# Average pooling of 33.55 MB: 2 KB per partition of the output stored from ScalarE's queue among the last loads

## The chip, the cores and the metric

The kernel runs on one core of one Trainium2 chip. The metric is device time in microseconds (us). A ratio is the mean time of one kernel's fast runs over that of the other's of the same rounds, so it is not quite the ratio of the medians that are quoted beside it.

## The reference

```python
def setup_inputs():
    batch, channels, d, h, w = (8, 32, 32, 32, 32)     # float32, kernel_size = 2
...
    for i, j, k in ...:                                # 16 x 16 x 16 windows
        window = x[:, :, 2*i:2*i+2, 2*j:2*j+2, 2*k:2*k+2]
        result[:, :, i, j, k] = np.mean(window, axis=(-3, -2, -1))
```

(The three loops are drawn together here.) The input is 33.55 MB, the output 4.19 MB. Each number is read once and takes part in one average, so the work is mostly movement.

## The kernel before

The 256 pairs of batch and channel are two halves (t = 0, 1) of 128 partitions. In each half a partition reads 128 KB and writes 16 KB. VectorE adds planes, then neighbours in a row, then rows, and scales by 1/8.

```python
    plan = [
        (0, 0, (32,)), (0, 32, (32,)), (0, 64, (32,)), (0, 96, (32,)),
        (1, 0, (32,)), (1, 32, (32,)), (1, 64, (16, 16)), (1, 96, (16, 16)),
    ]                                  # half, start in KB, sizes in KB per partition
...
    for t, k0, parts in plan:
        tin = pool_in.tile([P, 32 * KF], F32, tag="tin", name="tin")     # 5 buffers
        ...
            nc.sync.dma_start(out=v, in_=xv[...])       # 4 MB, or two of 2 MB ("half loads")
        for v, k, kb in views:
            pool_unit(v, t, k, kb)                      # three VectorE passes into obuf[t]

    for t, k0, kb in [(0, 0, 16), (1, 0, 14), (1, 14, 2)]:               # KB per partition
        nc.sync.dma_start(
            out=ov[t * P:(t + 1) * P, k0 * KF:(k0 + kb) * KF],
            in_=obuf[t][:, k0 * KF:(k0 + kb) * KF])
```

(The plan is set in fewer lines than in the source.) All ten loads and all three stores are issued by SyncE, on one queue. The closing part of the kernel, not shown, waits for the stores one by one.

Of the kernel before, what the change touches and what calls it, by code (L numbers as in the profile page):

```python
# [1 line left out]

# [4 lines left out]

F32 = mybir.dt.float32
KF = 256


@with_exitstack
def pool_rows(
    ctx: ExitStack,
    tc: tile.TileContext,
    x: bass.AP,
    kernel_size: int,
    out: bass.AP,
):
    nc = tc.nc  # L20
    assert kernel_size == 2, "only kernel_size == 2 supported"

    B, C, D, H, W = x.shape
    P = nc.NUM_PARTITIONS
    assert (B * C, D, H, W) == (2 * P, 32, 32, 32)
    add = mybir.AluOpType.add



    xv = x.rearrange("b c d h w -> (b c) (d h w)")  # L30
    ov = out.rearrange("b c d h w -> (b c) (d h w)")




    pool_in = ctx.enter_context(tc.tile_pool(name="pin", bufs=5))
    pool_out = ctx.enter_context(tc.tile_pool(name="pout", bufs=1))
    obuf = [pool_out.tile([P, 16 * KF], F32, name=f"obuf{t}") for t in range(2)]
    dummy = pool_out.tile([P, 1], F32, name="dummy")


    plan = [
        (0, 0, (32,)),
        (0, 32, (32,)),
        (0, 64, (32,)),
        (0, 96, (32,)),
        (1, 0, (32,)),
        (1, 32, (32,)),
        (1, 64, (16, 16)),
        (1, 96, (16, 16)),  # L50
    ]

    def pool_unit(buf, t, k0, kb):

        od = kb // 8
        a = buf.rearrange("p (o dd e) -> p o dd e", o=od, dd=2)
        b = buf[:, :od * 1024]
        nc.vector.tensor_add(  # L58
            out=b.rearrange("p (o e) -> p o e", o=od), in0=a[:, :, 0], in1=a[:, :, 1])
        bv = b.rearrange("p (e ww) -> p e ww", ww=2)  # L60
        c = buf[:, od * 1024:od * 1536]
        nc.vector.tensor_add(out=c, in0=bv[:, :, 0], in1=bv[:, :, 1])  # L62
        cv = c.rearrange("p (j hh k) -> p j hh k", hh=2, k=16)
        o0 = k0 * KF // 8
        nc.vector.tensor_tensor_reduce(  # L65
            out=obuf[t][:, o0:o0 + od * 256].rearrange("p (j k) -> p j k", k=16),
            in0=cv[:, :, 0], in1=cv[:, :, 1],
            scale=0.125, scalar=0.0, op0=add, op1=add, accum_out=dummy[:, :],
        )

    for t, k0, parts in plan:
        tin = pool_in.tile([P, 32 * KF], F32, tag="tin", name="tin")
        views = []
        o = 0
        for kb in parts:
            v = tin[:, o * KF:(o + kb) * KF]
            nc.sync.dma_start(
                out=v, in_=xv[t * P:(t + 1) * P, (k0 + o) * KF:(k0 + o + kb) * KF])
            views.append((v, k0 + o, kb))
            o += kb  # L80
        for v, k, kb in views:
            pool_unit(v, t, k, kb)


    for t, k0, kb in [(0, 0, 16), (1, 0, 14), (1, 14, 2)]:
        nc.sync.dma_start(
            out=ov[t * P:(t + 1) * P, k0 * KF:(k0 + kb) * KF],
            in_=obuf[t][:, k0 * KF:(k0 + kb) * KF],
        )


def kernel(tc: tile.TileContext, x: bass.AP, kernel_size: int, out: bass.AP):
    nc = tc.nc
    pool_rows(tc, x, kernel_size, out)
    tc.close()
    tc.compile()  # L96
    blocks = nc.main_func.blocks



    opening, program = blocks[0].instructions, blocks[tc.starting_block_idx].instructions
    load = next(i for i in program if isinstance(i, mybir.InstDMACopy))
    assert load.engine == nc.sync.engine
    barrier = next(
        n for n, i in enumerate(opening)
        if i.engine == load.engine and isinstance(i, mybir.InstDrain))
    program.remove(load)
    opening.insert(barrier, load)




    closing = blocks[-1].instructions
    stores = [
        i for i in program
        if isinstance(i, mybir.InstDMACopy) and "out_" in i.outs[0].memref]
    kept = [u.id for i in stores for u in i.sync_info.on_update]
    final = next(
        i for i in closing
        if i.engine == nc.sync.engine and isinstance(i, mybir.InstDrain))  # L120
    waits = {w.id: w for w in final.sync_info.on_wait}
    closing[closing.index(final)] = mybir.InstDrain(
        name=final.name, engine=final.engine, ins=[], outs=[], is_reset_sema=False,
        sync_info=mybir.SyncInfo(
            on_wait=[w for n, w in waits.items() if n not in kept], on_update=[]))


    reset = next(
        n for n, i in enumerate(closing)
        if isinstance(i, mybir.InstDrain) and i.is_reset_sema)  # L130
    first, stop = closing[reset].reset_range_start, closing[reset].reset_range_stop
    assert isinstance(closing[reset + 1], mybir.InstISA)
    while len(closing) > reset:
        closing.pop()
    n = first
    while n < stop:
        m = n
        while m < stop and m not in kept:
            m += 1
        if m > n:  # L140
            closing.append(mybir.InstDrain(
                name=nc.get_next_instruction_name(), engine=nc.gpsimd.engine, ins=[], outs=[],
                is_reset_sema=True, reset_range_start=n, reset_range_stop=m))
            nc.gpsimd.sem_clear(range(n, m))
        n = m + 1
    for n in kept:
        w = waits[n]
        closing.append(mybir.InstEventSemaphore(
            name=nc.get_next_instruction_name(), engine=nc.sync.engine, ins=[], outs=[],
            sync_info=mybir.SyncInfo(  # L150
                on_wait=[w],
                on_update=[mybir.SyncUpdate(
                    sync_type="semaphore", id=n, ant_name=w.ant_name,
                    update_mode="sem-sub-imm", update_value=w.wait_value)])))


# [1 line left out]
_INS = ['x', 'kernel_size']  # L158
_OUTS = [((8, 32, 16, 16, 16), 'float32')]

_NUMBERS = {'kernel_size': 2}


# [26 lines left out]
```

## Time and profile before

| what | value | where it is read |
|---|---|---|
| time | 91.97 us (91.76 to 92.02, 3 runs); 91.93 with the later ones (6 runs) | the runs |
| span of instructions | 86.4 us | head of the profile |
| transfer queue busy | 99.2% of 16 engines | queue table |
| VectorE busy | 74% | head of the profile |
| last store lands | 85.2 + 5.4 = 90.6 us | issues of the stores |

The span is the time from the first to the last instruction. A transfer goes on after the instruction that issues it, so the kernel ends later than its span. The prediction shows the lines themselves.

### The profile page before, as it was taken

Reading aid. Unit: us, or ns where it says so; the run is one execution under the profiler, and the core shown is the slowest. Engines: PE = TensorE matmul, PEld = TensorE weight load, DVE = VectorE, ACT = ScalarE, POOL = GpSimd, SP = SyncE. Lnnn points to the kernel's source line nnn. Section 1 sums busy time; section 2 is a strip of 40 time slices with the busy share of each in tenths; the row PEclk is TensorE's granted clock in tenths of the full one; section 3 lists DMA queues with packets and bytes.
Section 4 is the critical chain, followed back from the end, with each engine's and each line's share of the span. In section 5 each row is a group of like instructions: output and inputs, shape, how many; then the busy total and the mean of one; then the engine's idle time right before and its main releaser. Section 6 shows DMA issues by size and latency. Waiting matters only on the chain.

```text
span 86.4 us, 90 instructions
## 1 busy us (share of the span) xinstructions
DVE 64.0 (74%) x40; POOL 0.2 (0%) x4
## 2 busy tenths in 40 slices
DVE  0000039993999749993999749992999999999994
POOL 0000000000000000000000000000000000000000
DMA  8979997999979999799979999799999999998999
GB/s 243 425 319 470 486 470 319 425 486 486 455 319 440 486 486 410 319 486 486 470 319 425 486 486 440 304 470 387 455 402 455 395 455 410 440 425 319 448 432 408
DMA packets 1634, 36.37 MB, mean 421 GB/s; under 512 B 176, under 2 KB 176, under 8 KB 176
## 3 DMA queue, kind: packets, MB, share of 16 engines
q1 hardware_dynamic: 1634, 36.37, 99.2%
HBM read 33.55 MB, written 4.19 MB: 437 GB/s over the span
## 4 chain that ended last, share of the span: by engine, by line
DMA 61%; DVE 37%; issue 0%; DVEq 0%
DMA tin<-in_x_dram 61%; DVE tin L58 21%; DVE tin L62 11%; DVE obuf L65 6%; DVE dummy L65 0%; DVEq L96 0%
## 5 line engine op out<-in xcount | busy, mean ns | idle before, releaser
L58 DVE TENSOR_TENSOR tin<-tin 128x4096 f32<-128x4096 f32 (+1 forms) x10 | 35.7, 3569 | 20.6 <-DMA tin<-in_x_dram 20.6
L62 DVE TENSOR_TENSOR tin<-tin 128x2048 f32<-128x2048 f32 (+1 forms) x10 | 18.6, 1864 | 0.3
L65 DVE CUSTOM_DVE_ANT_1 obuf<-tin 128x1024 f32<-128x1024 f32 (+1 forms) x10 | 10.1, 1011 | 0.3
L65 DVE DVE_READ_ACCUMULATOR2_ANT dummy<- 128x1 f32 x10 | 0.8, 82 | 0.0
L171 POOL MEMSET const-bfloat16-1.0<- 128x1 bf16 x1 | 0.1, 102 | 0.0
L171 POOL MEMSET const-uint8-127<- 128x1 uint8 x1 | 0.1, 101 | 0.0
L171 POOL MEMSET const-float32-1.0<- 128x1 f32 x1 | 0.1, 99 | 0.0
L171 POOL MEMSET const-float32-0.0<- 128x1 f32 x1 | 0.1, 98 | 0.2 <-issue 0.2
## 6 DMA issues: line engine op xcount, KB each, us to landing
tin<-in_x_dram SPq DMA_DIRECT2D x6, 4096.0 KB, 34.9
tin<-in_x_dram SPq DMA_DIRECT2D x4, 2048.0 KB, 38.0
out_dram<-obuf SPq DMA_DIRECT2D x1, 2048.0 KB, 36.4
out_dram<-obuf SPq DMA_DIRECT2D x1, 1792.0 KB, 9.1
out_dram<-obuf SPq DMA_DIRECT2D x1, 256.0 KB, 5.4
```

Of the source, the lines that this page charges most:

```text
L58: nc.vector.tensor_add(out=b.rearrange("p (o e) -> p o e", o=od), in0=a[:, :, 0], in1=a[:, :, 1])
L62: nc.vector.tensor_add(out=c, in0=bv[:, :, 0], in1=bv[:, :, 1])
L65: nc.vector.tensor_tensor_reduce(out=obuf[t][:, o0:o0 + od * 256].rearrange("p (j k) -> p j k", k=16), in0=cv[:, :, 0], in1=cv[:, :, 1], s ...
L171: nc = _bacc.Bacc("TRN2", target_bir_lowering=False, num_devices=1)
```

## The change

A quarter of the second half's output is finished near 59 us but leaves only behind all loads, after 85 us. The intent is to let 2 KB per partition of it go at once, by another queue, while the loads still run, and so have that much less to store at the end.

```diff
-    for t, k0, kb in [(0, 0, 16), (1, 0, 14), (1, 14, 2)]:
-        nc.sync.dma_start(
+    for queue, t, k0, kb in [
+        (nc.scalar, 1, 0, 2),
+        (nc.sync, 0, 0, 16),
+        (nc.sync, 1, 2, 12),
+        (nc.sync, 1, 14, 2),
+    ]:
+        queue.dma_start(
...
     kept = [u.id for i in stores for u in i.sync_info.on_update]
+    kept = [n for j, n in enumerate(kept) if n not in kept[j + 1:]]
```

The last line takes doubles out of the list of semaphores that the closing part waits for. Here the four stores have four different semaphores, so it changes nothing.

## The prediction

> **What bounds the kernel now.** I read first the head of the page, because it says whether anything is idle for long, and what.
>
> ```profile
> span 86.4 us, 90 instructions
> DVE 64.0 (74%) x40; POOL 0.2 (0%) x4
> DMA packets 1634, 36.37 MB, mean 421 GB/s; under 512 B 176, under 2 KB 176, under 8 KB 176
> q1 hardware_dynamic: 1634, 36.37, 99.2%
> ```
>
> The one transfer queue is busy for 99.2% of what sixteen transfer engines can give over the span; VectorE (DVE) is busy for 74%. So bytes are the first suspect, though the chain of work that ended last speaks of VectorE near the end. Of its 39 pieces the big ones are these (start, duration, what):
>
> ```profile
> 20.15 40.47 DMA tin<-in_x_dram
> 60.63 0.02 issue
> 60.65 4.44 DVE tin L58
> ...
> 81.01 2.21 DVE tin L58
> 83.22 0.02 issue
> 83.25 1.24 DVE tin L62
> 84.48 0.02 issue
> 84.50 0.69 DVE obuf L65
> 85.20 0.01 DVEq L96
> ```
>
> Until 60.63 us the loads hold the chain, and from 60.65 to 85.20 VectorE works without a pause. This is not yet the end. The span closes with the last instruction, at 86.4 us, but that instruction only issues a store. Next, therefore, the issues of the stores (KB each, us from issue to landing), and when they are issued (in the chain and the timeline: 49.27, 81.0 and 85.2 us):
>
> ```profile
> out_dram<-obuf SPq DMA_DIRECT2D x1, 2048.0 KB, 36.4
> out_dram<-obuf SPq DMA_DIRECT2D x1, 1792.0 KB, 9.1
> out_dram<-obuf SPq DMA_DIRECT2D x1, 256.0 KB, 5.4
> ```
>
> They land at 49.27 + 36.4 = 85.7, 81.0 + 9.1 = 90.1 and 85.2 + 5.4 = 90.6 us. The measured 91.97 us is 1.4 us past that last landing. So the end is set by a transfer. Is that transfer late because its data were late, or because others stand before it? Adding issue and landing of the ten loads in the same way (narrow windows of the loads' tile) gives landings at 12.1, 21.8, 31.5, 41.2, 50.9, 60.6 for the six of 4 MB and 65.5, 70.4, 75.3, 80.8 for the four halves. That is one 4 MB load per 9.72 us: 4.194 MB / 9.72 us = 431.5 GB/s, without a step between them. The stretches towards the end show the same (us, DVE busy, POOL busy, clock, DMA share, GB/s):
>
> ```profile
> 60.00:65.00 5.00, 4.35 (x1) 0.00 (x0) 1.00 1.01 429
> 65.00:70.00 5.00, 4.96 (x4) 0.00 (x0) 1.00 1.00 426
> 75.00:80.00 5.00, 4.93 (x5) 0.00 (x0) 1.00 1.03 393
> 80.00:85.00 5.00, 4.90 (x6) 0.00 (x0) 1.00 0.99 425
> 86.00:88.00 2.00, 0.00 (x0) 0.00 (x0) 1.00 1.00 430
> 88.00:89.00 1.00, 0.00 (x0) 0.00 (x0) 1.00 0.88 377
> 89.00:90.00 1.00, 0.00 (x0) 0.00 (x0) 1.00 0.69 266
> ```
>
> The DMA share stays at 1.0 from the first load to 88 us, loads and stores alike, and falls only in the last two. The queue works strictly in order: the first store, ready at 49.27, waits behind all loads and lands 4.9 us after the last of them. The whole kernel is a single stream of 33.55 + 4.19 = 37.75 MB. Check: 37.75 MB / 431.5 GB/s = 87.5 us, plus a head of 12.1 - 9.7 = 2.4 us, is 89.9, and the rest up to 90.6 is the thinner end of the last store. **The bound is the byte stream, to the very end**; VectorE runs beside it.
>
> **What the Trainium skill says.** "DMA: Bandwidth & Descriptors", section "Issuing engines are not separate DMA queues": DMAs begun by different engines end up on the same 16 DMA engines and interleave; a second issuer saves only the time of issuing. The trace before has one queue alone and can't show it, but it shows that issuing costs little: a store's instruction takes 332 to 347 ns. The same page, "Where 436 GB/s comes from", puts the ceiling at 435.2 GB/s; my 431.5 GB/s is 99% of it, so the trace agrees and leaves no room for an overlap. The same page, "Queues, rings and completion order": each DMA engine takes turns between its queues, a packet at a time. No run so far shows it; I use it for where the moved bytes land in the stream. "Perfetto Trace Analysis", section "DMA Instruction — HWDGE (DVE, Sync)": the profiled window of such an instruction leaves out the movement of data. The trace agrees: about 0.34 us for the first store's instruction, 36.4 us to its landing.
>
> **The change, part by part.** The order of instructions of the changed kernel shows VectorE's forty instructions as before, the same ten loads, one new transfer of 128x512 on ScalarE, and SyncE's second store cut from 128x3584 to 128x3072. Semaphores shift by one slot; the new slots' earlier owners are loads 3, 4 and 5, which land at 41.2, 50.9 and 60.6, before the stores are due at 49.3, 81.0 and 85.2. So no new wait there.
>
> *Removed*: 2 KB from each of the second store's 128 rows. Each of the sixteen engines has eight rows: 8 x 2 KB = 16.4 KB at 431.5/16 = 27.0 GB/s is **0.61 us less** in the tail.
>
> *Added*: 128 packets of 2 KB on ScalarE's queue. What does such a packet cost? The last store is made of them. From 88 us to the end the trace has 187 packets of 0.65 MB, at 39.8% of 16 engines over 4 us = 25.5 engine-us. By bytes these are 27 rows of 14 KB, 128 of 2 KB and 32 tiny ones (completions). The 27 take 27 x 0.53 = 14.4, which leaves 11.1 for the rest; in 89.9 to 90.3 us, 12 packets, seven of them of 2 KB, take 0.63. The two together give about 85 ns per 2 KB and 8 ns per completion. Eight per engine: 8 x 0.085 + 0.008 = **0.69 us more**, as an estimate from these windows.
>
> *Moved*: this store waits for the unit that ends at about 58.95 us, so it is issued at 59.0 and its packets start near 60.5 (the first load's packets appear some 1 us after its issue). From there it stands between the packets of the half loads. A 16 KB row takes 0.61 us, so eight turns of 0.61 + 0.085 are 5.6 us: it should land at about 66.5, some 6 to 9 us after issue. The half loads land 0.6 to 0.7 us later, at about 66.2, 71.1, 76.0 and 81.5. VectorE wants them at 67.32, 72.54, 76.73 and 80.93 (its adds in the timeline): the first three still come in time, and the fourth makes it wait 0 to 0.6 us. The last store is then issued at 85.2 to 85.8. The queue ahead of it has work until some 89 us, so this delay is hidden as well.
>
> *Sum on the stream that sets the end*: -0.61 + 0.69 = +0.08 us; a fourth store's completion to wait for in the closing part, already there by then, about 0.02 us (the small "issue" pieces of the chain). 91.97 + 0.10 = 92.07. What was taken out of the tail has been put in front of it, in the same stream.
>
> **The rivals.** *A: the store is hidden among the loads.* Reads and writes of device memory may use different paths, so the 256 KB would ride for free and the tail be 0.6 us shorter: 91.97 - 0.61 = 91.4. For it: this seems to be the intent, and the tail is all stores while the middle is all loads, so the profile shows no mixed stretch. Against it: loads alone (429) and stores alone (425 to 430) run at the same rate with the share at 1.0, which looks like a limit of the engines and not of a direction. I give it 15 to 20%.
>
> *B: the mixing costs.* Short writes between long reads may slow the reads, or the turns between queues leave gaps. If the 4.9 us that the store spends among loads ran at 393 GB/s, the slowest stretch seen, instead of 429, it would lose 4.9 x (429/393 - 1) = 0.45 us: 92.5. Against it: the page shows no gap at the seams between DMAs. 10 to 15%.
>
> *C: VectorE becomes the bound.* The fourth half load has only 0.1 us of slack, so delays pass into VectorE's chain and the last store. The end moves only if that store's packets come to the engines after the stream has run dry near 89 us. A store that starts moving 1.0 to 1.5 us after issue must be issued after 87.5; that takes 2.3 us of delay, more than three times the estimate. If it did happen, each further us would count in full. 5%.
>
> **Range and chances.** The sum gives 92.07; A pulls a little below it, so I say **92.0 us**. The range goes from A with a little more (91.3) to B in full with some scatter (92.6); the three runs of before span 0.26 us. A change of 2% is 1.84 us, three times all the bytes that are moved, so faster by over 2% has 1%, slower by over 2% has 2% (C, or a cost of the second queue outside the profile), and within 2% has **97%**.
>
> **What would show it right or wrong.** Right: a second queue with 144 packets and 0.26 MB in the profile; the new store landing 6 to 9 us after an issue near 59 us; half loads landing 0.6 to 0.7 us later, VectorE's last unit starting up to 0.6 us later and the span longer by as much (86.4 to 87.1 us), yet the time the same; the DMA share at 1.0 up to some 88 us. Were A right, the half loads would land when they did before, with more than 435 GB/s for a while after 60.5 us, and the last landing would come near 90.0. Were B right, the stretches from 60 to 70 us would show under 420 GB/s with both queues in them. The prediction is wrong if the last landing moves from 90.6 us by more than 0.6 us either way.

## The result, and the profile after

The changed kernel takes **91.77 us** (91.55 to 91.79, 6 runs) against 91.93 us (91.76 to 92.09, 6 runs). The ratio is 0.9979, with a 95% interval from 0.9962 to 0.9995: the same at 2%, and perhaps 0.2% better.

The head and the queue table of the profile after:

```profile
span 86.6 us, 91 instructions
DMA packets 1774, 36.48 MB, mean 421 GB/s; under 512 B 192, under 2 KB 192, under 8 KB 320
q1 hardware_dynamic: 1630, 36.22, 98.4%
q10 hardware_dynamic: 144, 0.26, 0.8%
```

The second queue is there with the 144 packets expected: 128 rows and 16 completions. Mean rate and span are nearly those of before. Next the issues of the stores after (KB, us from issue to landing); the timeline has the issues at 49.3, 81.1, 59.0 and 85.5 us:

```profile
out_dram<-obuf SPq DMA_DIRECT2D x1, 2048.0 KB, 36.8
out_dram<-obuf SPq DMA_DIRECT2D x1, 1536.0 KB, 8.8
out_dram<-obuf ACTq DMA_DIRECT2D x1, 256.0 KB, 9.9
out_dram<-obuf SPq DMA_DIRECT2D x1, 256.0 KB, 4.9
```

ScalarE's store lands at 59.0 + 9.9 = 68.9 us. The other three land at 86.1, 89.9 and 90.4 us, where they landed at 85.7, 90.1 and 90.6 before. So the first store is 0.4 us later and the end is 0.2 us earlier, and the time follows the end. The four half loads land at 66.2, 71.3, 76.2 and 81.2 us, which is 0.6, 0.9, 0.9 and 0.4 us later than before. The chain of work that ended last says the same of the fourth:

```profile
39.96 41.20 DMA tin<-in_x_dram
...
81.18 2.30 DVE tin L58
```

VectorE now waits for this half load, until 81.18 us, where before it was never idle after 60.65 us. Last, the stretches (us, DVE busy, POOL busy, clock, DMA share, GB/s):

```profile
60.00:65.00 5.00, 4.33 (x1) 0.00 (x0) 1.00 1.03 411
65.00:70.00 5.00, 4.97 (x4) 0.00 (x0) 1.00 0.97 412
75.00:80.00 5.00, 4.93 (x5) 0.00 (x0) 1.00 1.02 429
88.00:89.00 1.00, 0.00 (x0) 0.00 (x0) 1.00 0.97 412
89.00:90.00 1.00, 0.00 (x0) 0.00 (x0) 1.00 0.64 244
```

Where ScalarE's store runs, the rate fell from 429 and 426 to 411 and 412 GB/s. From 75 to 80 us it rose from 393 to 429 GB/s. That second difference was not foreseen: no byte was taken out of this stretch.

**Packet records.** The trace also has the start and duration of every packet. One packet is one row of one partition, and every store or load has eight rows on each of the 16 engines. The usual (median) durations are the same in both kernels:

```
row of  2 KB    84 ns        row of 14 KB   535 ns
row of 12 KB   460 ns        row of 16 KB   611 to 613 ns
completion       9 ns
```

The 16 KB rows are not all alike. In the kernel before, 35 of them take 41 to 568 ns longer than the 612 ns, and all of these start between 76.9 and 79.1 us, in the last half load. I add up what every 16 KB row takes over 612 ns and divide by 16; I call this the **excess** per engine. Before it is 0.61 us, nearly all in that slow stretch. After it is 0.40 us: 0.32 between 60 and 64 us and only 0.07 near 78 us.

So the experiments had to settle three things: whether the gain is real, whether it comes from bytes that ride for nothing, from the cut of the store, from the second queue, or from the slow stretch, and what the slow stretch hangs on.

### The profile page after: what moved, and what is told of

Same layout as the page of the kernel before. It is cut to its first block, busy times and chain, and to the rows that moved or that the text cites. A ratio compares the mean times of both kernels' runs of the same rounds, so it can differ in the third digit from the quotient of the medians.

```text
span 86.6 us, 91 instructions
## 1 busy us (share of the span) xinstructions
DVE 64.1 (74%) x40; POOL 0.2 (0%) x4
## 4 chain that ended last, share of the span: by engine, by line
DMA 83%; DVE 14%; SPq 1%; issue 0%; DVEq 0%
DMA tin<-in_x_dram 83%; DVE tin L58 8%; DVE tin L62 4%; DVE obuf L65 2%; SPq L77 1%; DVE dummy L65 0%; DVEq L102 0%
```

## The experiments

Four theories. **Same stream**: what leaves the tail costs as much among the loads. **Partly hidden**: reads and writes overlap a little. **Ends better**: shorter rows or two queues make the tail more even. **Slow stretch**: the gain is a slow stretch of reads that has become smaller. All kernels gave correct results. In the fences from here on, each line is one stretch with the columns as above.

### before_again: the kernel before against itself

> The kernel before against itself: shows what five rounds can resolve, and gives a second trace of it. All theories: ratio 1.000, interval within 0.2% of 1. 'Scatter' theory: the stretch of slow read packets between 77 and 79 us (0.59 us per engine in the first trace) is of another size or place in this trace, and the last landing shifts with it by up to 0.4 us. 'Own property' theory: the stretch is there again, same place, same size.

91.99 us (6 runs) against 92.04 us, ratio 0.9991, interval 0.9971 to 1.0011.

```profile
75.00:80.00 5.00, 4.93 (x5) 0.00 (x0) 1.00 1.00 380
```

The slow stretch is there again: excess 0.63 us, from 76.8 us on, and the last landing is again at 90.6 us. It belongs to this kernel. Five rounds resolve about 0.2%.

### after_again and after_third: the changed kernel repeated

> The changed kernel repeated. 'Same stream' theory (moved bytes cost in the loads what they save in the tail): ratio 0.999 to 1.002, the 0.998 of the first measurement was scatter. 'Partly hidden' theory and 'ends better' theory (the tail of the stores ends more evenly): 0.998 again, with the interval clear of 1. In the trace: half loads again 0.5 to 0.9 us later, last landing 0.1 to 0.3 us earlier.

> The changed kernel a third time, for its ratio and a third trace. 'Slow stretch' theory: ratio 0.997 to 0.999; the trace's excess in 16 KB packets (0.39 us per engine at 91.76 us, 0.61 at 91.96) goes with this profiled run's time, about 0.2 us of time per 0.2 us of excess. 'Same stream' alone: 0.999 to 1.001, no such relation.

Measured: 91.81 us against 92.04, ratio 0.9972 (0.9954 to 0.9990); and 91.90 us against 91.99, ratio 0.9991 (0.9974 to 1.0008), this one on another chip. Of the first repetition, then of the second:

```profile
60.00:65.00 5.00, 4.42 (x1) 0.00 (x0) 1.00 0.96 406
...
75.00:80.00 5.00, 4.93 (x5) 0.00 (x0) 1.00 1.02 387
```

```profile
60.00:65.00 5.00, 4.21 (x1) 0.00 (x0) 1.00 0.99 387
...
75.00:80.00 5.00, 4.93 (x5) 0.00 (x0) 1.00 1.00 429
```

Two of three measurements have intervals clear of 1, and the third leans the same way: a gain of 0.1 to 0.3%. The slow stretch is not the same in all three traces. In the first repetition it is whole (excess 0.64 us, 0.56 of it after 78 us), and that profiled run, at 91.96 us, is the slowest of its six. In the second it is gone, with 0.38 us of excess at 60 to 64 us instead; there slow reads began earlier, with another 0.29 us in 32 KB rows between 46 and 60 us, which the excess as defined above leaves out. The expectation that this trace's time would go with its excess missed: 0.39 us took 91.90 us here, and 0.40 us took 91.76 us in the first trace. The lines of 60 to 65 us above must be read with care: packets are counted whole, and one 16 KB packet more or less is 3.3 GB/s of a 5 us line. The excess is the better measure.

### split_sp: the cut of the store alone, on SyncE's queue

```diff
-        (nc.scalar, 1, 0, 2),
         (nc.sync, 0, 0, 16),
+        (nc.sync, 1, 0, 2),
         (nc.sync, 1, 2, 12),
```

(This diff and those of act_4k, act_early, act_tail, act_16k and late_first are against the changed kernel; the others are against the kernel before.)

> The changed kernel's four pieces, but the 2 KB piece stays on SyncE's queue, between the first and the second store, so it is not among the loads: the cut alone, without the second queue. 'Ends better' theory (shorter rows of 12 KB in the second store, later last store): most of the gain stays, 0.998 to 0.999. 'Partly hidden' theory: no gain, and the 0.08 us of the eight short packets more per engine: 1.000 to 1.002. 'Same stream': 1.001.

92.06 us against 92.04, ratio 0.9994 (0.9974 to 1.0013): no gain that can be told from none. Against the changed kernel of the same rounds it is 0.20 us slower (means of six runs 92.01 and 91.81 us).

```profile
75.00:80.00 5.00, 4.93 (x5) 0.00 (x0) 1.00 1.00 374
```

The slow stretch is whole (excess 0.71 us). Shorter rows in the tail are not the gain, or at most a part of it.

### act_tail: the second queue alone, in the tail

```diff
-        (nc.scalar, 1, 0, 2),
         (nc.sync, 0, 0, 16),
-        (nc.sync, 1, 2, 12),
+        (nc.scalar, 1, 0, 14),
         (nc.sync, 1, 14, 2),
```

> ScalarE's queue used in the tail only: the whole second store (14 KB rows) on ScalarE beside SyncE's first and last stores; nothing is among the loads. 'Second queue' theory (two queues side by side end more evenly or leave fewer gaps, wherever they are used): 0.996 to 0.999. 'Slow stretch' and 'partly hidden': no gain, 0.999 to 1.002, slow stretch there.

92.17 us against 91.97, ratio 1.0012 (0.9989 to 1.0035), excess 0.56 us in the usual place. A second queue is not in itself a gain. With split_sp, this takes away **ends better** as far as cut or queue were to bring it.

### act_4k: twice the dose

```diff
-        (nc.scalar, 1, 0, 2),
+        (nc.scalar, 1, 0, 4),
         (nc.sync, 0, 0, 16),
-        (nc.sync, 1, 2, 12),
+        (nc.sync, 1, 4, 10),
```

> Twice the dose: 4 KB per partition on ScalarE's queue, second SyncE store 10 KB. 'Partly hidden' theory: twice the gain of the change, about 0.996 (0.4 us). 'Same stream': 0.999 to 1.001, half loads up to 1.3 us later, VectorE's last unit starts about 1 us later than in the kernel before, end unmoved. 'Ends better': same as the change, 0.998.

91.77 us against 92.04, ratio 0.9967 (0.9948 to 0.9985); the changed kernel had 0.9972 in the same rounds. Twice the bytes did not give twice the gain, though the intervals would not exclude it.

```profile
60.00:65.00 5.00, 4.36 (x1) 0.00 (x0) 1.00 1.00 395
...
75.00:80.00 5.00, 4.91 (x5) 0.00 (x0) 1.00 1.02 436
```

This trace has no slow stretch after 76 us and 0.38 us of excess from 60 to 66 us, like two of the three of the changed kernel.

### act_early: the same bytes, but among the early loads

```diff
-        (nc.scalar, 1, 0, 2),
-        (nc.sync, 0, 0, 16),
-        (nc.sync, 1, 2, 12),
+        (nc.scalar, 0, 0, 2),
+        (nc.sync, 0, 2, 14),
+        (nc.sync, 1, 0, 14),
```

> The same 2 KB per partition on ScalarE's queue, but of the first half of the output, so it is issued at about 20 us, among the 4 MB loads, not in the last third; the first SyncE store is 14 KB, the second 14 KB. 'Slow stretch' theory (the gain is that the stretch of slow reads near 77 to 79 us, about 0.6 us per engine in three traces of kernels without the change, is smaller when short writes have gone among the half loads just before): no gain here, ratio 1.000 to 1.002, stretch still in the trace. 'Partly hidden' theory: gain as in the change, 0.997 to 0.998, since any place among the loads will do.

91.88 us against 91.97, ratio 0.9987 (0.9966 to 1.0007): not told apart from none, nor from half the gain.

```profile
75.00:80.00 5.00, 4.90 (x6) 0.00 (x0) 1.00 0.99 367
```

The slow stretch is whole (excess 0.68 us). ScalarE's store itself ran without a slow stretch of its own: it starts at 23.8 us, and the 32 KB rows about it show at most 0.03 us of excess. Had the bytes ridden for nothing, the loads after them would not have moved. They did: the sixth load landed at 61.3 us, against 60.6 before, 0.7 us later. **Partly hidden** has nothing left for it here.

### act_16k: eight times the dose, the whole first store

```diff
-        (nc.scalar, 1, 0, 2),
-        (nc.sync, 0, 0, 16),
-        (nc.sync, 1, 2, 12),
+        (nc.scalar, 0, 0, 16),
+        (nc.sync, 1, 0, 14),
```

> Eight times the dose: the whole first store (16 KB per partition, 2 MB) on ScalarE's queue from 49.3 us. 'Partly hidden' in proportion: up to 1.6 us faster, 0.983. 'Same stream' with rival C: all later loads land up to 4.9 us later, VectorE's last unit ends near 90 us, the last store then meets a dry queue and lands near 92.5: 93.5 to 94.3 us, ratio 1.017 to 1.025.

93.71 us against 91.97, ratio 1.0188 (1.0163 to 1.0212), inside what **same stream** with rival C gave. Its stores (KB, us to landing), the last two issued at 85.9 and 90.1 us:

```profile
out_dram<-obuf ACTq DMA_DIRECT2D x1, 2048.0 KB, 18.3
out_dram<-obuf SPq DMA_DIRECT2D x1, 1792.0 KB, 5.8
out_dram<-obuf SPq DMA_DIRECT2D x1, 256.0 KB, 2.3
```

The last half load landed at 39.9 + 45.9 = 85.8 us, against 80.8 before: 5 us later for 2 MB, the full price of the bytes. VectorE ended at 90.1 us and the last store landed at 92.4 us, with a queue that had run short of work. Bytes do not ride for nothing, and a large dose makes VectorE the bound. In this kernel no store stands behind the loads, and the 16 KB rows have no excess at all; the loads near the start of ScalarE's store have 0.94 us of it, between 50 and 54 us.

### extra_load: is the slow stretch a matter of time?

```diff
     plan = [
         (0, 0, (32,)),
+        (0, 0, (32,)),
```

> The kernel before with the first 4 MB unit loaded and computed twice (same result): everything after it comes 9.7 us later, time about 101.7 us. Asks what the slow stretch at 77 to 79 us hangs on. If on time since the start: it stays at 77 to 79 us. If on the place in the program (the last half load, ahead of the first store): it comes at 86.5 to 89 us.

101.36 us (2 runs). These are two stretches of it:

```profile
75.00:80.00 5.00, 5.00 (x3) 0.00 (x0) 1.00 1.03 439
...
85.00:90.00 5.00, 4.89 (x6) 0.00 (x0) 1.00 0.99 397
```

From 75 to 80 us the rate is full. The slow stretch has moved by about the 9.7 us, to 86.4 to 88.9 us, though it is smaller (0.30 us). It hangs on the place in the program, not on time.

### swap: is it a matter of the bytes read?

```diff
-        (1, 64, (16, 16)),
         (1, 96, (16, 16)),
+        (1, 64, (16, 16)),
```

> The kernel before with its last two units loaded and computed in the other order, so the last half load reads other bytes (third quarter of the second half); the second store then waits for all of VectorE, to about 85.2 us, and the time may be a little longer (92 to 93). Asks only for the stretch. If it hangs on the bytes that the last half load read: it moves to the half load of those bytes, near 67 to 69 us, or is gone. If on the last place ahead of the stores: still 76.8 to 79 us.

93.05 us (one run, state unknown; a look only, and the longer time was expected).

```profile
75.00:80.00 5.00, 4.93 (x5) 0.00 (x0) 1.00 1.01 387
```

The slow stretch stays where it was, with other bytes in the last half load (excess 0.62 us). It goes with the last place ahead of the stores.

### late_first: no store behind the loads until 76.8 us

```diff
-        (nc.scalar, 1, 0, 2),
-        (nc.sync, 0, 0, 16),
-        (nc.sync, 1, 2, 12),
-        (nc.sync, 1, 14, 2),
+        (nc.sync, 1, 0, 12),
+        (nc.sync, 0, 0, 16),
+        (nc.sync, 1, 12, 4),
```

> No second queue. SyncE's first store is now the 12 KB rows that are ready at about 76.75 us, then the 16 KB rows of the first half, then 4 KB rows at the end: so no store stands in the queue behind the loads until some 76.8 us, where the slow stretch began before. If the stretch hangs on a store waiting behind the last load: none from 76.8 to 78, little after it, last landing about 0.3 to 0.6 us earlier, ratio 0.994 to 0.998. If it hangs on the last load's place or bytes alone: stretch as before, ratio 0.999 to 1.001.

**91.42 us** (91.30 to 91.80, 6 runs) against 91.99, ratio 0.9946 (0.9925 to 0.9967): faster than both kernels, with one queue and three stores. First its last half load's stretch, then its stores, issued at 77.2, 76.8 and 85.2 us in this order:

```profile
75.00:80.00 5.00, 4.93 (x5) 0.00 (x0) 1.00 1.00 426
```

```profile
out_dram<-obuf SPq DMA_DIRECT2D x1, 2048.0 KB, 11.5
out_dram<-obuf SPq DMA_DIRECT2D x1, 1536.0 KB, 7.0
out_dram<-obuf SPq DMA_DIRECT2D x1, 512.0 KB, 4.7
```

The slow stretch is gone (excess 0.11 us in all, 0.02 of it from 78 to 80 us). The last store lands at 89.9 us, 0.7 us earlier than before. Its 460 and 159 ns rows take as long together as the 535 and 84 ns of before, so nothing was won there. VectorE's line is the same in both kernels too (4.93 us, x5), so its work alone is not what slows the reads. What was won is 0.5 us of excess, and a more even end: the mean of the last store's sixteen completions was 0.38 us ahead of the last of them before, and is 0.18 us here. That second term is no safe property of a kernel: gate, below, which stores as the kernel before does, has 0.18 us as well.

### gate: a test that failed

```diff
             pool_unit(v, t, k, kb)
+            if (t, k) == (1, 80):
+                nc.vector.tensor_copy(out=obuf[0][:, 0:1], in_=obuf[0][:, 0:1])
```

late_first changed two things: when the first store is issued, and which rows go first. This run was to change the first alone.

> The kernel before with one thing more: after the second half of unit 6, at about 76.75 us, VectorE copies one column of the first half's result onto itself, so that the first store (same rows, same order of stores) can't be issued before some 76.8 us instead of 49.3. It costs VectorE about 0.1 us. If the slow stretch hangs on a store that has been waiting in the queue behind the loads: no stretch, ratio 0.993 to 0.997, like the run with the late rows first. If it was the order or the size of the rows that helped there: stretch from 76.8 us as before, ratio 0.999 to 1.002.

91.86 us against 91.94, ratio 0.9988 (0.9969 to 1.0006). It tests nothing: the scheduler put the copy at the earliest place that its data allowed, after the first unit near 20 us, and the first store was issued at 49.3 us as always. It is one more trace of the kernel before, its slowest:

```profile
75.00:80.00 5.00, 4.93 (x5) 0.00 (x0) 1.00 0.99 354
```

### The excess and the time, over all traces

Each profiled run with its excess in the 16 KB rows and its own time, apart from swap, extra_load and act_16k, whose ends are set otherwise:

```
late_first   0.11  91.30      act_tail      0.56  91.95      act_early  0.68  92.02
act_4k       0.38  91.63      before        0.61  91.99      split_sp   0.71  92.12
after_third  0.39  91.90      before_again  0.63  92.00      gate       0.83  92.21
after        0.40  91.76      after_again   0.64  91.96
```

A straight line through these has 1.2 us of time for 1 us of excess (correlation 0.96 over 11 traces). Counting the 32 KB rows after 12 us as well, over their usual 1213 ns, adds 0.31 us to after_third, 0.26 to gate, 0.10 to act_early and 0.04 to 0.07 to the others; the line then has 1.0 us for 1 us (correlation 0.94), and after_third no longer stands off it. So the times of these executions go with how long slow reads went on. This is a correlation; it does not show what makes the reads slow.

The starts of the packets show one thing more, over all fourteen traces. In twelve of them the main group of slow reads begins 2.1 to 3.3 us before the first row of a store behind or among these reads: 76.9 against 79.8 us before, 60.4 against 62.6 (ScalarE's store) after, 50.3 against 53.1 in act_16k. In after_third it begins long before, near 48.8 us, and late_first has none. The stretch at 60 to 64 us and the one at 77 to 79 us may thus be one thing, ahead of one store or of another; that is not shown.

## Why the prediction was right, and where it was not

The number held: 92.0 us said, 91.77 us measured (91.81 and 91.90 in the repetitions), within 91.3 to 92.6, and nothing near 2%. The single steps:

- **The byte stream as the bound: right.** Half loads came 0.4 to 0.9 us later for 256 KB, where 0.6 to 0.7 was worked out (the fourth came least late, because before it was itself held up by the slow stretch). act_early moved the loads by 0.7 us for the same bytes, and act_16k by 5 us for eight times as many.
- **The cost of the packets: right.** Removed were 8 x (535 - 460) ns = 0.60 us, where 0.61 was said. Added were 8 x 84 + 9 ns = 0.68 us, where 0.69 was said. The sum is +0.08 us, as predicted.
- **When ScalarE's store lands: wrong.** 9.9 us after issue, not 6 to 9. The turns took about what was worked out, 5.3 us from the first row's start to the last one's end, against 5.6. What failed is "its packets start near 60.5": the first was recorded at 62.6 us, 3.6 us after issue. In all seven traces with a store on ScalarE beside a full SyncE queue this delay is 3.5 to 3.9 us, so that of the first load in an idle machine (about 1 us) was the wrong measure.
- **VectorE's slack: right.** It waited 0.25 us more (81.18 against 80.93), the span grew by 0.2 us, and both stayed hidden. Rival C came true only with act_16k, at 93.71 us.
- **The sum: wrong in sign, by 0.2 to 0.4 us.** It said +0.10 us; the means of the three measurements are -0.20, -0.26 and -0.07 us. The step that failed is "Sum on the stream that sets the end": it took the rest of the stream as unchanged. The prediction's own landings speak against its words "without a step between them": the last half load lands 5.5 us after the third, the others 4.9 us apart. This is the slow stretch, 0.6 us long. The 393 GB/s from 75 to 80 us stood in the profile as well, and I used it only as "the slowest stretch seen", to size rival B. What the runs put in place of an unchanged stream are two terms that change from one execution to the next. Mean excess of the three traces after is 0.48 us, of the two before 0.62: -0.14 us; with the 32 KB rows it is 0.61 against 0.66, only -0.04. The last store's completions end more closely together, 0.26 us from mean to last against 0.38: -0.12 us. With +0.08 for the packets this makes -0.18 us, or -0.08 with the 32 KB rows, where the last landing of these traces came 0.12 us earlier on average. That it fits is no proof: gate, in effect the kernel before, has 1.08 us of excess with the 32 KB rows and 0.18 us from mean to last, so both terms scatter within one kernel as much as they differ between the two.
- **Luck.** The 92.0 us lies nearer to the result than the sum's 92.07, but it was lowered for rival A, which did not come true.
- **Rival A (hidden) has fallen: the loads moved, as the first point says.** Its sign of over 435 GB/s does stand in a line (449 from 70 to 75 us), but the third half load landed 4.87 us after the second there and 4.90 us before, so this is the counting of whole packets. **Rival B (mixing costs) is half right**: 0.3 to 0.4 us of excess at 60 to 64 us in two of three traces, where 0.45 was allowed for; but in these the later stretch was nearly or wholly gone.

Shown: the stretch follows the place ahead of the stores (extra_load, swap); it is gone when no store is issued before 76.8 us and other rows go first (late_first), and from the last half load when none stands behind it (act_16k, where 0.94 us came about the start of ScalarE's store instead); neither the cut nor the second queue alone was seen to bring the gain (split_sp, act_tail). **Open**: whether late_first works because no store waits behind the loads, or by the order and size of its rows, since the gate did not gate; where the changed kernel's 0.1 to 0.3% come from, since with all rows counted only one of its three traces has clearly less excess than before (0.47 us, against 0.68 and 0.69); why the late stretch was nearly or wholly gone in two of them and whole in the third; and what in the machine makes these reads slow.

## What to carry to other kernels

In this kernel, bound by its byte stream, a store that was moved ahead paid among the loads about what it saved at the end: in such a kernel, look for the gain in stretches where the same bytes take longer, not in the order alone. A line of the profile that is 8% under its neighbours is a finding, not a scale for a rival: compare it over repeated traces before predicting. After adding an instruction that is only there to delay another, read the order that the scheduler made of it.

## What the Trainium skill lacked or had wrong

- "DMA: Bandwidth & Descriptors" has nothing on reads that slow down ahead of stores in the same queue: 354 to 393 GB/s over five microseconds in the kernels with the first store queued at about 50 us and nothing from ScalarE among the half loads, against 426 GB/s when the first store was issued at 76.8 us.
- The same page, "Queues, rings and completion order", tells how an engine takes turns between queues. The turns agree, one row each: 119 of the 16 KB rows start between the first and the last of ScalarE's 128 rows. That a second queue's first packet comes only 3.5 to 3.9 us after its issue when the first queue is full, it does not say.
- I found no page with measured times of single packets of such lengths. The traces have 84 ns for 2 KB, 159 for 4 KB, 460 for 12 KB, 535 for 14 KB and about 612 for 16 KB.
